# A matmul with leaky ReLU: a plain first unit, one ordered ring of rounding loads, stores on ScalarE, and two regions that take turns

## The chip, the cores and the metric

The kernel runs on one core of one Trainium2 chip; the other cores are idle. The metric is device time in microseconds (us), as the median of repeated runs.

## The reference

```python
def reference(a, b, alpha):          # a, b: 4096 x 4096 fp32, alpha 0.01
    x = np.matmul(a, b)
    return np.where(x > 0, x, alpha * x)
```

## The kernel before

The output is cut into regions of 512 x 1024 elements, 32 in all. A region fills the kernel's eight accumulator banks (4 row blocks `mt` by 2 column halves `nt`) and takes four units of 1024 along k, each of 8 slices `c`: 64 matmuls of 128x128 by 128x512 per unit and region, 8192 in all. Two regions in a row (`h` = 0, 1) share the same B. The kernel transposes A and rounds both inputs to bf16.

A came by GpSimd, whose transfers round on the way, and was transposed by VectorE. B came as fp32 over Sync's queue and was rounded by ScalarE (first region) or VectorE. Stores were issued by GpSimd too:

```python
    def load_a(mb, h, sub, mp):
        ...                                   # (cut) 256 rows of A, one unit
        for q in range(4):
            src = a[row:row + 2 * P, k0 + q * w:k0 + (q + 1) * w]
            nc.gpsimd.dma_start(a16[32 * q:32 * q + 32], src.rearrange("(g i) w -> i g w", i=32))
        ...
        nc.vector.transpose(dst..., a16...)   # (cut)

    def load_b(pi, n, sub, c, scalar=False):
        ...
        nc.sync.dma_start(b32, src[:, c, :])
        if scalar:
            nc.scalar.copy(bt[pi, u][:, c0 + c, :], b32)
        else:
            nc.vector.tensor_copy(bt[pi, u][:, c0 + c, :], b32)
    ...
    # end of a row block in the first two regions
                nc.gpsimd.dma_start(place(0, h, pairs[0], mt), o)
```

`TURNS = [[0, 1, 2, 3, 4]]` meant that the first region ran through all of k before the second began.

## Time and profile before

| | before |
|---|---|
| time, median of 3 runs | 1828.29 us (1827.49 to 1829.02) |
| span of the profiled run | 1825.7 us |

The prediction below reads the profile: only the first 140 us have room.

### The profile page before, as it was taken

The page shows a single profiled execution, that of the slowest core. Times are in us where ns is not written, and L with a number is a line of the kernel's source. Part 1 is how long each engine was busy: PE and PEld are TensorE (multiplying, and loading weights), DVE is VectorE, ACT ScalarE, POOL GpSimd, SP SyncE. Part 2 cuts the span into 40 slices and gives each one's busy share as a digit, 9 for nine tenths or more (in the row PEclk, how much of TensorE's full clock was granted, in tenths as well). Part 3 has the DMA queues.
Part 4 walks back from the last instruction along what each step waited for, and adds up shares of the span by engine and source line. Part 5 has one row for each costly group of instructions (what it writes and reads, how often), then busy time and mean ns, then how long its engine had stood idle before and what let it go on. Part 6 is the DMA issues. An engine that isn't in the chain of part 4 may idle for free.

```text
span 1825.7 us, 18868 instructions
## 1 busy us (share of the span) xinstructions
PE 1776.4 (97%) x8041; PEld 804.5 (44%) x8204; DVE 475.6 (26%) x465; ACT 174.3 (10%) x290; POOL 253.6 (14%) x448
## 2 busy tenths in 40 slices
PE   5789999999999999999999999999999999999999
PEld 2334444444444444444444444444444444444444
DVE  1454231214442213022452312201255130311000
ACT  5200000000000000000000000000000000000001
POOL 3150000033310000003520000001242000000000
PEclk7899999999999999999999999999999999999999
DMA  9799773465585629155856835617387581644111
GB/s 325 181 162 352 270 272 143 181 141 101 100 235 210 230 105 338 65 196 81 131 100 230 289 126 198 263 64 226 62 111 198 203 337 46 244 171 160 70 46 47
DMA packets 166037, 320.04 MB, mean 175 GB/s; under 512 B 46657, under 2 KB 95809, under 8 KB 165953
## 3 DMA queue, kind: packets, MB, share of 16 engines
q1 hardware_dynamic: 61056, 220.23, 33.0%
q0 software_dynamic: 104896, 98.59, 24.7%
q8 instruction: 64, 1.05, 0.2%
q14 instruction: 21, 0.16, 0.0%
HBM read 285.21 MB, written 67.11 MB: 193 GB/s over the span
## 4 chain that ended last, share of the span: by engine, by line
PE 93%; DMA 4%; issue 2%; POOL 1%; DVE 0%; ACT 0%; POOLq 0%; DVEq 0%
PE ps L101 93%; DMA a<-in_a_dram 4%; POOL a L81 0%; POOL out_dram L233 0%; DVE at L83 0%; ACT o L288 0%; DVEq L83 0%; POOLq L81 0%; POOLq L233 0%; POOLq L310 0%
## 5 line engine op out<-in xcount | busy, mean ns | idle before, releaser
L101 PE MATMUL ps<-bt,at 128*128 128x512 bf16 x8029 | 1772.1, 381 | 43.4 <-DVE at L83 34.7
L101 PEld LDWEIGHTS <-at 128*128 128x128 bf16 x8192 | 803.0, 98 | 1012.5 <-DVE at L83 40.2
L98 DVE CAST bt<-b 128x1024 bf16<-128x1024 f32 x384 | 256.6, 691 | 851.9 <-PE ps L101 553.0
L83 DVE STREAM_TRANSPOSE at<-a 128x2048 bf16<-128x2048 bf16 (+1 forms) x80 | 219.4, 2779 | 365.1 <-DMA a<-in_a_dram 241.9
L288 ACT ACTIVATE o<-ps 128x512 f32<-128x512 f32 x240 | 130.7, 595 | 1524.1 <-PE ps L101 1408.2
L292 POOL DMA_DIRECT2D out_dram<-o x116 | 64.5, 556 | 1364.8 <-ACT o L288 1355.8
L81 POOL DMA_DIRECT2D a<-in_a_dram x320 | 183.4, 587 | 83.4 <-DMA a<-in_a_dram 50.5
L96 ACT CAST bt<-b 128x1024 bf16<-128x1024 f32 x32 | 33.4, 1045 | 26.1 <-DMA b<-in_b_dram 26.1
L232 ACT ACTIVATE o<-ps 128x512 f32<-128x512 f32 x16 | 8.7, 594 | 97.4 <-PE ps L101 87.9
L233 POOL DMA_DIRECT2D out_dram<-o x8 | 5.5, 687 | 66.5 <-ACT o L232 66.5
L126 PE MATMUL ps<-w 128*128 128x512 bf16 x12 | 4.3, 532 | 2.3 <-ACT w L123 2.3
L126 PEld LDWEIGHTS <-w 128*128 128x128 bf16 x12 | 1.5, 131 | 4.6 <-ACT w L123 2.3
L123 ACT ACT_TABLE_LOAD x1 | 1.3, 1283 | 0.7 <-PEq L310 0.7
L122 DVE MEMSET w<- 128x256 uint32 x1 | 0.3, 272 | 0.9 <-PEq L310 0.9
L123 ACT ACTIVATE w<-w 128x8 bf16<-128x8 bf16 x1 | 0.2, 208 | 0.0
L310 POOL MEMSET const-float32-0.0<- 128x1 f32 x1 | 0.1, 98 | 0.2 <-issue 0.2
L310 POOL MEMSET const-bfloat16-1.0<- 128x1 bf16 x1 | 0.1, 101 | 0.0
L310 POOL MEMSET const-float32-1.0<- 128x1 f32 x1 | 0.1, 98 | 0.0
L310 POOL MEMSET const-uint8-127<- 128x1 uint8 x1 | 0.1, 98 | 0.0
## 6 DMA issues: line engine op xcount, KB each, us to landing
b<-in_b_dram SPq DMA_DIRECT2D x416, 512.0 KB, 5.4
out_dram<-o POOLq DMA_DIRECT2D x124, 512.0 KB, 2.9
a<-in_a_dram POOLq DMA_DIRECT2D x192, 128.0 KB, 5.1
a<-in_a_dram POOLq DMA_DIRECT2D x128, 64.0 KB, 3.3
out_dram<-o SPq DMA_DIRECT2D x8, 256.0 KB, 2.0
```

What stands on the lines that cost most here:

```text
L81: nc.gpsimd.dma_start(a16[32 * q:32 * q + 32], src.rearrange("(g i) w -> i g w", i=32))
L83: nc.vector.transpose(dst.rearrange("p c (g i) -> p g c i", g=8), a16.rearrange("p g (j c) -> p g c j", c=kc))
L96: nc.scalar.copy(bt[pi, u][:, c0 + c, :], b32)
L98: nc.vector.tensor_copy(bt[pi, u][:, c0 + c, :], b32)
L101: nc.tensor.matmul(ps, at[mb, h, u][:, c, mt * P:(mt + 1) * P], bt[pi, u][:, c, nt * NT:(nt + 1) * NT], start=first, stop=last,)
L123: nc.scalar.activation(w[:, :8], w[:, :8], LRELU, alpha=alpha)
L126: nc.tensor.matmul(wp, w[:, :P], w, start=True, stop=True)
L232: nc.scalar.activation(o[:, nt * NT:(nt + 1) * NT], done, LRELU, alpha=alpha)
L233: nc.gpsimd.dma_start(place(0, h, pairs[0], mt), o)
L288: nc.scalar.activation(o[:, cols], banks[mt, nt], LRELU, alpha=alpha)
L292: nc.gpsimd.dma_start(to, o)
L310: nc = _bacc.Bacc("TRN2", target_bir_lowering=False, num_devices=1)
```

## The change

Its intent: A and B share one queue, that of GpSimd, called the ring here, in the order in which they are needed; "plain" is a load that doesn't round; the first unit comes plain over Sync at once, its A turned by TensorE; the first two regions take turns over k, so that the same bytes feed twice the matmuls; stores leave GpSimd.

```diff
-TURNS = [[0, 1, 2, 3, 4]]
+TURNS = [[0], [1], [2, 3]]
...
     def load_b(...):
-        nc.sync.dma_start(b32, src[:, c, :])
-        ... ScalarE or VectorE rounds b32 into bt
+        nc.gpsimd.dma_start(new_b(pi, u)[:, c, :], b_rows(n, u, c))
...
+    order = [("a", 0), ("b", 0), ("a", 1), ("b", 1), ("b", 2), ("a", 2), ...]   # first unit, on nc.sync
+    def take(what, i):
+        if what == "b":
+            nc.scalar.copy(b0[:, i, :], b_in[i // 4][:, i % 4, :])
+            return
+        nc.vector.tensor_copy(a_rounded[:, i, :], a_in[:, i, :])
+        for c in range(KC):
+            nc.tensor.transpose(turned[i, c // 4][:, c % 4, :], cols[:, c, :], ident)
+        nc.scalar.copy(a0[:, :4, i * P:(i + 1) * P], turned[i, 0])
+        nc.vector.tensor_copy(a0[:, 4:, i * P:(i + 1) * P], turned[i, 1])
...
+        if (what, i) == ("b", 3):
+            nc.gpsimd.tensor_copy(x[:, :1], b0[:, 2, :1])      # GpSimd's loads start after this
...
+            if last:
+                todo = [(quarter, c) for c in range(KC)]
+            else:
+                todo = [(mt, c) for c in (2 * quarter, 2 * quarter + 1) for mt in range(MT)]
...
-                nc.gpsimd.dma_start(place(0, h, pairs[0], mt), o)
+            nc.scalar.dma_start(place(0, h, pairs[0], mt), o)
...
-                        nc.gpsimd.dma_start(to, o)
+                        nc.scalar.dma_start(to, o)
```

At the end of a turn the partial sums go to SBUF (`spill`), in the first turn as copies by ScalarE (`nt` = 0) and VectorE (`nt` = 1), later as VectorE adds. The first two regions become eight steps of 64 matmuls each. Left out of the cut above: the number of buffers changes (5 for 4 of A's loads, 5 for 6 of B's units), A's first pieces are larger, and the warm-up has 8 matmuls for 12.

More of the change, by code (lines that the diff above doesn't have):

```diff
@@ L6 @@
 from concourse._compat import with_exitstack
+from concourse.masks import make_identity
 P = 128
@@ L45 @@
     alpha = float(alpha)
-    KU = K // (KC * P)
+    KW = KC * P
+    KU = K // KW
     RM = MT * P
     RN = NP * NT
+    QW = KW // 4
     HALVES = 2
@@ L52 @@
     NB = N // RN
-    subs = [(0, 0, 4, 0), (0, 4, 4, 512)] + [(u, 0, 8, 1024 * u) for u in range(1, KU)]
-    subs_of = {u: [s for s in subs if s[0] == u] for u in range(KU)}
+    assert TURNS[0] == [0] and sorted(sum(TURNS, [])) == list(range(KU))
+    small_pool = ctx.enter_context(tc.tile_pool(name="small", bufs=1))
     at_pool = ctx.enter_context(tc.tile_pool(name="at", bufs=HALVES * KU))
-    bt_pool = ctx.enter_context(tc.tile_pool(name="bt", bufs=KU + 2))
-    a16_pool = ctx.enter_context(tc.tile_pool(name="a16", bufs=4))
@@ L61 @@
-    b32_pool = ctx.enter_context(tc.tile_pool(name="b32", bufs=4))
+    bt_pool = ctx.enter_context(tc.tile_pool(name="bt", bufs=KU + 1))
+    part_pool = ctx.enter_context(tc.tile_pool(name="part", bufs=2))
+    a16_pool = ctx.enter_context(tc.tile_pool(name="a16", bufs=5))
     o_pool = ctx.enter_context(tc.tile_pool(name="oo", bufs=2))
-    warm_pool = ctx.enter_context(tc.tile_pool(name="warm", bufs=1))
     psum_pool = ctx.enter_context(tc.tile_pool(name="psum", bufs=8, space=bass.MemoryType.PSUM))
+    ident = small_pool.tile([P, P], BF16, name="ident")
@@ L66, with new_a @@
+    make_identity(nc, ident)
     ctx.enter_context(tc.manual_schedule())
+    w = small_pool.tile([P, NT], BF16, name="w")
+    nc.vector.memset(w, 0.0)
+    x = small_pool.tile([P, 8], FP32, name="x")
+    nc.vector.memset(x, 0.0)
+    nc.scalar.activation(x, x, LRELU, alpha=alpha)
+    wp = psum_pool.tile([P, NT], FP32, name="ps")
+    for _ in range(8):
+        nc.tensor.matmul(wp, w[:, :P], w, start=True, stop=True)
     at = {}
     bt = {}
-    def load_a(mb, h, sub, mp):
-        u, c0, kc, k0 = sub
+    def new_a(mb, h, u):
@@ L74, in load_a @@
         if (mb, h, u) not in at:
             at[mb, h, u] = at_pool.tile([P, KC, RM], BF16, name="at")
-        row = (mb * HALVES + h) * RM + 2 * mp * P
-        w = 32 * kc
-        a16 = a16_pool.tile([P, 8, w], BF16, name="a16")
-        for q in range(4):
-            src = a[row:row + 2 * P, k0 + q * w:k0 + (q + 1) * w]
-            nc.gpsimd.dma_start(a16[32 * q:32 * q + 32], src.rearrange("(g i) w -> i g w", i=32))
-        dst = at[mb, h, u][:, c0:c0 + kc, 2 * mp * P:2 * (mp + 1) * P]
@@ L83, in load_a, with new_b @@
-        nc.vector.transpose(
-            dst.rearrange("p c (g i) -> p g c i", g=8), a16.rearrange("p g (j c) -> p g c j", c=kc)
-        )
-    def load_b(pi, n, sub, c, scalar=False):
-        u, c0, kc, k0 = sub
+        return at[mb, h, u]
+    def new_b(pi, u):
         if (pi, u) not in bt:
             bt[pi, u] = bt_pool.tile([P, KC, RN], BF16, name="bt")
-        b32 = b32_pool.tile([P, RN], FP32, name="b32")
-        src = b[k0:k0 + kc * P, n * RN:(n + 1) * RN].rearrange("(p c) n -> p c n", c=kc)
-        nc.sync.dma_start(b32, src[:, c, :])
-        if scalar:
-            nc.scalar.copy(bt[pi, u][:, c0 + c, :], b32)
-        else:
-            nc.vector.tensor_copy(bt[pi, u][:, c0 + c, :], b32)
+        return bt[pi, u]
@@ new lines, in load_a @@
+    def load_a(mb, h, u, mp):
+        dst = new_a(mb, h, u)[:, :, 2 * mp * P:2 * (mp + 1) * P]
+        row = (mb * HALVES + h) * RM + 2 * mp * P
+        a16 = a16_pool.tile([P, 8, QW], BF16, name="a16")
+        for q in range(4):
+            src = a[row:row + 2 * P, u * KW + q * QW:u * KW + (q + 1) * QW]
+            nc.gpsimd.dma_start(a16[32 * q:32 * q + 32], src.rearrange("(g i) w -> i g w", i=32))
+        nc.vector.transpose(
+            dst.rearrange("p c (g i) -> p g c i", g=8), a16.rearrange("p g (j c) -> p g c j", c=KC)
+        )
@@ L100, in mm, with b_rows, load_b @@
+    def b_rows(n, u, c):
+        src = b[u * KW:(u + 1) * KW, n * RN:(n + 1) * RN]
+        return src.rearrange("(p c) n -> p c n", c=KC)[:, c, :]
+    def load_b(pi, n, u, c):
+        nc.gpsimd.dma_start(new_b(pi, u)[:, c, :], b_rows(n, u, c))
     def mm(ps, mb, h, pi, u, mt, nt, c, first, last):
@@ L118, in place @@
         return out[row:row + P, n * RN:(n + 1) * RN]
-    w = warm_pool.tile([P, NT], BF16, name="w")
-    nc.vector.memset(w, 0.0)
-    nc.scalar.activation(w[:, :8], w[:, :8], LRELU, alpha=alpha)
-    wp = psum_pool.tile([P, NT], FP32, name="ps")
-    for _ in range(12):
-        nc.tensor.matmul(wp, w[:, :P], w, start=True, stop=True)
     regions = []
@@ L142 @@
         for u in range(KU):
-            pieces = [
-                lambda pi=pi, sub=sub, c=c: load_b(pi, pairs[pi], sub, c)
-                for sub in subs_of[u]
-                for c in range(sub[2])
-            ]
             lead = 2 if pi == 1 else KU
-            loads.setdefault(first * KU + u - lead, []).extend(pieces)
+            loads.setdefault(first * KU + u - lead, []).extend(
+                lambda pi=pi, u=u, c=c: load_b(pi, pairs[pi], u, c) for c in range(KC)
+            )
     for mb in range(1, MB):
@@ L153 @@
             for u in range(KU):
-                pieces = [
-                    lambda mb=mb, h=h, sub=sub, mp=mp: load_a(mb, h, sub, mp)
-                    for sub in subs_of[u]
-                    for mp in range(MT // 2)
-                ]
-                loads.setdefault(first * KU + h * KU + u - 2 * KU + 1, []).extend(pieces)
-    def issue(slot, part):
-        pieces = loads.get(slot, [])
-        for piece in pieces[len(pieces) * part // 4:len(pieces) * (part + 1) // 4]:
+                loads.setdefault(first * KU + h * KU + u - 2 * KU + 1, []).extend(
+                    lambda mb=mb, h=h, u=u, mp=mp: load_a(mb, h, u, mp) for mp in range(MT // 2)
+                )
@@ L165, in issue, with quarter_of, step_loads @@
+    def quarter_of(pieces, quarter):
+        for piece in pieces[len(pieces) * quarter // 4:len(pieces) * (quarter + 1) // 4]:
             piece()
     steps = [
-        (t, h, sub, i == len(turn) - 1)
+        (t, h, u, i == 0, i == len(turn) - 1)
         for t, turn in enumerate(TURNS)
         for h in range(HALVES)
-        for i, sub in enumerate(turn)
+        for i, u in enumerate(turn)
     ]
-    def step_loads(t, h, si):
-        sub = subs[si]
+    def step_loads(h, u):
         if h:
-            return [lambda mp=mp: load_a(0, 1, sub, mp) for mp in range(MT // 2)]
-        order = "abbabb" if sub[2] == 4 else "abbbabbbbb"
-        made, na, nb = [], 0, 0
-        for what in order:
-            if what == "a":
-                made.append(lambda mp=na: load_a(0, 0, sub, mp))
-                na += 1
-            else:
-                made.append(lambda c=nb: load_b(0, pairs[0], sub, c, True))
-                nb += 1
-        return made
@@ L190 @@
-    queue = [step_loads(t, h, si) for t, h, si, _ in steps]
-    part = {}
-    if len(TURNS) > 1:
-        for piece in queue[0]:
-            piece()
-        queue[0] = []
-    banks = None
-    for i, (t, h, si, last) in enumerate(steps):
-        u, c0, kc, _ = subs[si]
-        for piece in queue[i]:
-            piece()
-        following = queue[i + 1] if i + 1 < len(steps) else []
-        queue[i] = []
-        if si == TURNS[t][0]:
-            banks = new_banks()
-        def go(mt, c):
-            for nt in range(NP):
-                mm(banks[mt, nt], 0, h, 0, u, mt, nt, c0 + c, si == TURNS[t][0] and c == 0,
-                   last and c == kc - 1)
-        def spill(mt):
-            if not last:
-                return
-            for nt in range(NP):
-                ps = banks[mt, nt]
-                if len(TURNS) == 1:
-                    continue
-                if h not in part:
-                    part[h] = bt_pool.tile([P, MT, NP, NT], FP32, name="part", tag="bt")
-                kept = part[h][:, mt, nt, :]
-                if t == 0:
-                    if h == 0 and nt:
-                        nc.vector.tensor_copy(kept, ps)
-                    else:
-                        nc.scalar.copy(kept, ps)
-                else:
-                    nc.vector.tensor_add(kept, ps, kept)
-            if t == len(TURNS) - 1:
-                o = o_pool.tile([P, RN], FP32, name="o")
-                for nt in range(NP):
-                    done = banks[mt, nt] if len(TURNS) == 1 else part[h][:, mt, nt, :]
-                    nc.scalar.activation(o[:, nt * NT:(nt + 1) * NT], done, LRELU, alpha=alpha)
-                nc.gpsimd.dma_start(place(0, h, pairs[0], mt), o)
-        def ahead(quarter):
-            for piece in following[len(following) * quarter // 4:len(following) * (quarter + 1) // 4]:
-                piece()
-        extra = len(steps) - 2
-        if i == 0:
-            for mts, cs in (((0, 1), (0, 1)), ((2, 3), (0, 1)), ((0, 1, 2, 3), (2, 3))):
-                for c in cs:
-                    for mt in mts:
-                        go(mt, c)
-            for quarter in range(4):
-                ahead(quarter)
-                spill(quarter)
-        elif last:
-            for mt in range(MT):
-                for c in range(kc):
-                    go(mt, c)
-                spill(mt)
-                ahead(mt)
-                if i >= extra:
-                    issue(2 * KU - 2 + i - extra, mt)
-        else:
-            for quarter in range(4):
-                for c in range(kc * quarter // 4, kc * (quarter + 1) // 4):
-                    for mt in range(MT):
-                        go(mt, c)
-                ahead(quarter)
-                if i >= extra:
-                    issue(2 * KU - 2 + i - extra, quarter)
-        if i + 1 < len(steps):
-            queue[i + 1] = []
@@ new lines, in step_loads, with spill @@
+            return [lambda mp=mp: load_a(0, 1, u, mp) for mp in range(MT // 2)]
+        made = [lambda c=c: load_b(0, pairs[0], u, c) for c in range(KC)]
+        made.insert(4, lambda: load_a(0, 0, u, 1))
+        made.insert(0, lambda: load_a(0, 0, u, 0))
+        return made
+    queue = [step_loads(h, u) for _, h, u, _, _ in steps]
+    part = {}
+    def spill(t, h, mt, banks):
+        for nt in range(NP):
+            kept = part[h][:, mt, nt * NT:(nt + 1) * NT]
+            if t == 0:
+                if nt:
+                    nc.vector.tensor_copy(kept, banks[mt, nt])
+                else:
+                    nc.scalar.copy(kept, banks[mt, nt])
+            else:
+                nc.vector.tensor_add(kept, banks[mt, nt], kept)
+        if t == len(TURNS) - 1:
+            o = o_pool.tile([P, RN], FP32, name="o")
+            nc.scalar.activation(o, part[h][:, mt, :], LRELU, alpha=alpha)
+            nc.scalar.dma_start(place(0, h, pairs[0], mt), o)
@@ new lines @@
+    a_in = bt_pool.tile([P, MT, KW], FP32, name="a_in", tag="bt")
+    b_in = [part_pool.tile([P, KC // 2, RN], FP32, name="b_in", tag="part") for _ in range(2)]
+    a_rounded = at_pool.tile([P, MT, KW], BF16, name="a_rounded", tag="at")
+    order = [("a", 0), ("b", 0), ("a", 1), ("b", 1), ("b", 2), ("a", 2), ("b", 3), ("a", 3),
+             ("b", 4), ("b", 5), ("b", 6), ("b", 7)]
+    for what, i in order:
+        if what == "a":
+            nc.sync.dma_start(a_in[:, i, :], a[i * P:(i + 1) * P, :KW])
+        else:
+            nc.sync.dma_start(b_in[i // 4][:, i % 4, :], b_rows(pairs[0], 0, i))
@@ new lines @@
+    a0 = new_a(0, 0, 0)
+    b0 = new_b(0, 0)
+    turned = {
+        (mt, i): psum_pool.tile([P, KC // 2, P], BF16, name="turned", tag="ps")
+        for mt in range(MT)
+        for i in range(2)
+    }
+    banks = new_banks()
+    def take(what, i):
[3 more added lines that the diff above has]
+        nc.vector.tensor_copy(a_rounded[:, i, :], a_in[:, i, :])
+        cols = a_rounded[:, i, :].rearrange("m (p c) -> m c p", c=KC)
+        for c in range(KC):
+            nc.tensor.transpose(turned[i, c // 4][:, c % 4, :], cols[:, c, :], ident)
+        nc.scalar.copy(a0[:, :4, i * P:(i + 1) * P], turned[i, 0])
+        nc.vector.tensor_copy(a0[:, 4:, i * P:(i + 1) * P], turned[i, 1])
@@ new lines @@
+    there = {"a": [], "b": []}
+    ready = []
+    begun = set()
+    for n, (what, i) in enumerate(order):
+        take(what, i)
+        if (what, i) == ("b", 3):
+            nc.gpsimd.tensor_copy(x[:, :1], b0[:, 2, :1])
+        there[what].append(i)
+        now = [(i, c) for c in there["b"]] if what == "a" else [(mt, i) for mt in there["a"]]
+        ready.append(now)
+        for mt, c in ready[n - 1] if n else []:
+            for nt in range(NP):
+                mm(banks[mt, nt], 0, 0, 0, 0, mt, nt, c, (mt, nt) not in begun, False)
+                begun.add((mt, nt))
@@ new lines @@
+    for piece in queue[1]:
+        piece()
+    part[0] = part_pool.tile([P, MT, RN], FP32, name="part", tag="part")
+    for mt, c in ready[-1]:
+        for nt in range(NP):
+            mm(banks[mt, nt], 0, 0, 0, 0, mt, nt, c, False, True)
+        spill(0, 0, mt, banks)
+    for piece in queue[2]:
+        piece()
+    for i in range(1, len(steps)):
+        t, h, u, first, last = steps[i]
+        following = queue[i + 1] if 2 <= i and i + 1 < len(steps) else []
+        own = 2 * KU - 2 + i - (len(steps) - 2)
+        if first:
+            banks = new_banks()
+            if h not in part:
+                part[h] = part_pool.tile([P, MT, RN], FP32, name="part", tag="part")
+        for quarter in range(4):
+            if last:
+                todo = [(quarter, c) for c in range(KC)]
+            else:
+                todo = [(mt, c) for c in (2 * quarter, 2 * quarter + 1) for mt in range(MT)]
+            for mt, c in todo:
+                for nt in range(NP):
+                    mm(banks[mt, nt], 0, h, 0, u, mt, nt, c, first and c == 0,
+                       last and c == KC - 1)
+            if last:
+                spill(t, h, quarter, banks)
+            quarter_of(following, quarter)
+            if own >= 2 * KU - 2:
+                quarter_of(loads.get(own, []), quarter)
@@ L276 @@
                 if final and last:
-                    order = [(c, nt) for nt in range(NP) for c in range(KC)]
+                    todo = [(c, nt) for nt in range(NP) for c in range(KC)]
                 else:
-                    order = [(c, nt) for c in range(KC) for nt in range(NP)]
-                for c, nt in order:
+                    todo = [(c, nt) for c in range(KC) for nt in range(NP)]
+                for c, nt in todo:
                     mm(banks[mt, nt], mb, h, pi, u, mt, nt, c, u == 0 and c == 0,
@@ L291 @@
                     if not final:
-                        nc.gpsimd.dma_start(to, o)
-                issue(r * KU + u, mt)
+                        nc.scalar.dma_start(to, o)
+                quarter_of(loads.get(r * KU + u, []), mt)
 _INS = ['a', 'b', 'alpha']
```

## The prediction

The sum came to 25 us lost: 16.2 ahead of the second step, and three terms, estimates of 3.0 us ahead of the fifth step, 4.3 ahead of the seventh and 1.5 for the half clock after it. In the 30.3 us for the second step, 0.3 and 0.7 are estimates as well; the kernel before has 0.69 us for a cast on VectorE.

> **What bounds the kernel now.** I read the page's totals and slices first, then the table of windows, the timeline of TensorE and the list of waits over the first 140 us.
>
> ```profile
> span 1825.7 us, 18868 instructions
> ...
> PE   5789999999999999999999999999999999999999
> PEld 2334444444444444444444444444444444444444
> ...
> PEclk7899999999999999999999999999999999999999
> ```
>
> Each digit is the busy share of 1/40 of the span (45.6 us). Only the first three slices are not full: nothing can be won in the other 37. The table of windows (columns: PE busy and count, PEld busy and count, DVE, ACT, POOL, granted clock, DMA share, GB/s) puts a number on it:
>
> ```profile
> 0.00:140.00 140.00, 102.44 (x404) 42.55 (x413) 56.89 (x27) 39.26 (x42) 48.33 (x88) 0.85 0.94 223
> 140.00:1826.00 1686.00, 1673.93 (x7639) 761.94 (x7791) 418.72 (x439) 135.02 (x248) 205.24 (x360) 1.00 0.55 171
> ...
> 400.00:600.00 200.00, 199.06 (x910) 90.60 (x927) 79.11 (x58) 14.67 (x28) 43.83 (x77) 1.00 0.65 162
> ```
>
> I count weight loads, because some matmul records are missing: 927 in 200 us is 0.2157 us per matmul. The 8192 matmuls need 8192 x 0.2157 = 1767 us. The first 140 us hold 413 loads less 12 of the warm-up = 401, worth 86.5 us, so **53.5 us are lost there**. After 140 us 7791 loads are worth 1680.5 of 1685.7 us: 5.2 us, nearly all of it the tail after the last matmul. 1767 + 53.5 + 5.2 = 1825.7, the span. The change can win back at most the 53.5 us, and in practice not the wait for the first data.
>
> What TensorE waits for there, from its timeline (start, duration, then in brackets the idle time before and its releaser):
>
> ```profile
> 12.20 3.58 PE L101 MATMUL ps<-bt,at 128*128 128x512 bf16 x8 [5.63 <-DVE at L83]
> 18.34 7.90 PE L101 MATMUL ps<-bt,at 128*128 128x512 bf16 x28 [2.56 <-DVE at L83]
> ...
> 43.42 1.89 PE L101 MATMUL ps<-bt,at 128*128 128x512 bf16 x4 [3.90 <-DVE at L83]
> 54.50 16.70 PE L101 MATMUL ps<-bt,at 128*128 128x512 bf16 x63 [9.20 <-DVE at L83]
> ...
> 108.22 32.06 PE L101 MATMUL ps<-bt,at 128*128 128x512 bf16 x137 [6.13 <-DVE at L83]
> ```
>
> VectorE is only the messenger. It transposes A and itself waits for A's transfers, as the waits of that window say:
>
> ```profile
> DVE at L83 <- DMA a<-in_a_dram: 82.2, 13, 19.4
> POOL a L81 <- DMA a<-in_a_dram: 46.2, 25, 2.9
> ```
>
> So A is starved while B flows on the other queue. In the timeline the ScalarE casts of B between 20 and 60 us follow each other every 1.65 us (512 KB, 318 GB/s), while the transposes of A start at 39.55, 50.63, 62.45 us: 1 MB of fp32 per 11.5 us, about 90 to 105 GB/s. B takes three to four times A's share, and A is needed first. Also, one region needs 24 MB for 55 us of matmuls, while two regions need 32 MB for 110 us: with one region at a time the DMA is the limit, with two it is not.
>
> [...] B's packets are 4 KB and A's 1 KB of source, and the bytes divide about 3 or 4 to 1. One ring removes this. [...] after the 9.20 us of idle the matmuls at 54.50 us come 0.43 us apart until 60.0 us; after a 1.7 us gap at 72.91 us they stay at 0.216. [...]
>
> **The change, part by part.**
>
> *Casts of B.* 384 on VectorE (256.6 us) and 32 on ScalarE (33.4 us) go. From 140 us on TensorE waits for neither: worth nothing in the steady part. Matmuls and their order there stay as they were: 1767 us.
>
> *B by GpSimd's ring.* Can the ring carry it? A's rounding loads alone moved 192 GB/s written between 120 and 125 us, 384 GB/s read, and the plain B loads 359 GB/s between 140 and 200 us. I take 360 GB/s read for both: a B row is 4 KB in and 2 KB out, no smaller than A's pieces, so I see no reason for less. Issue costs 0.57 us of GpSimd each, 512 KB per 1.46 us at that rate: hidden.
>
> *First unit plain, on Sync.* 6 MB in 12 transfers of 512 KB at 1.4 us each, first landing about 4.2 us (the first cast of the old kernel starts at 4.55). VectorE rounds A (0.69 us), TensorE does 32 transposes. Matmuls follow arrivals, cold at first. The order of instructions on GpSimd shows that the ring starts only after ScalarE has copied the third B slice: landing 9.8 us plus 1.05 us and a queue behind A's copies, about 12 us. From then it shares with the last four or five plain loads, at 1.65 us each: the plain unit is in at 20.6 us. TensorE has 64 x 0.216 = 13.8 us of matmuls[...] from 7.8 us on, some cold: I put its end at 27 us.
>
> *Second step (other half of A, same B).* The ring's first 1 MB gets about 105 GB/s until 20.6 us and is in at 21.7. The instruction order on VectorE puts both transposes of 3.82 us (row 128x2048) ahead of its copies of the first partial sums, and TensorE needs the first such copy for a free bank: 21.7 + 0.3 + 7.6 + 0.7 = 30.3, so **step 2 begins at about 30 us** where ideally it is 13.8: 16.2 us lost.
>
> *Further steps.* 64 matmuls are 13.8 us each, eight steps in all. Step 3 starts at 44: its 6 MB stand behind the second 2 MB (in at 24.5), so in at 24.5 + 17.5 = 42: just in time. After that the ring needs 8 MB / 0.36 = 23.3 us per unit against 27.6 us of matmuls and runs ahead. What is left is VectorE, which works in program order. In step 4 (counting from one) it has eight adds[...] and three transposes: one left over from step 3, two for step 5. [...] At the end of step 6 the last add[...] is followed by a transpose that step 7 needs for its fifth matmul[...]. Steps 2 to 4 otherwise find their data.
>
> *Stores* move from GpSimd (0.556 us each) to ScalarE, 0.60 us x 2 of work per 3.45 us: off the path.
>
> [...] Span 1767 + 25 + 5.2 = 1797.2; the old kernel's time exceeds its span by 2.6 us, so about **1800 us**; I choose 1799. The gain is 29 us of the 53.5, 1.6%.
>
> **Rivals.** *(a) VectorE does not hold TensorE up:* if the copies and adds end early enough, or the ring gets more than a quarter beside Sync so that step 2 begins at 27, only 13 to 15 us are lost: 1767 + 14 + 5.2 + 2.6 = 1789. For: VectorE is busy only 26% now. Against: the instruction order. *(b) The rounding B loads are slow,* say 250 GB/s read. Then the 21 MB of steps 3 to 8 that follow 24.5 us, with A at 360, take about 76 us instead of 58, and the last B unit lands near 105 us rather than 85, when step 6 wants it at 89: 15 us more, 1815. For: the trace of before holds no such transfer. Against: A's smaller pieces run at 384. *(c) The ring in order becomes a bound later,* a store or A load blocking B: B then is asked for four units (55 us) ahead and takes 16 MB / 0.36 = 46 us, and the A loads of the next rows fall in regions that load no B. I expect nothing, at worst a few us.
>
> **Range and chances.** 2% faster begins at 1828.3 / 1.02 = 1792.4; it needs the losses to be 18 us or less, that is rival (a). My central value is 7 us above; I give it 0.25. Slower needs over 90 us of loss: 0.02. Range 1788 to 1809: (a) whole on one side, half of (b) on the other.
>
> **What would show it.** Right: weight loads 0.216 us apart from 140 us on; no releaser "DMA b" on TensorE after the first unit; TensorE idle ahead of steps 2, 5 and 7 with VectorE as releaser[...]; first 64 matmuls done at 25 to 29 us; DMA share high until about 100 us. Wrong: TensorE waiting for B's transfers in steps 3 to 6 (the ring's rate), or gaps after 140 us (the ring's order), or no gaps ahead of steps 5 and 7 (my reading of VectorE's list).

## More of the kernel before

One more view of the kernel before matters for what follows, and the prediction did not use it: the timeline of GpSimd around the end of the first region. The columns are start, duration, engine, line, operation and tiles, count, and in brackets the idle time before and what ended it; L233 is the output store, L81 the loads of A.

```profile
90.69 0.57 POOL L233 DMA_DIRECT2D out_dram<-o  x1 [20.90 <-ACT o L232]
94.14 0.55 POOL L233 DMA_DIRECT2D out_dram<-o  x1 [2.88 <-ACT o L232]
94.69 2.32 POOL L81 DMA_DIRECT2D a<-in_a_dram  x4
...
101.10 0.55 POOL L233 DMA_DIRECT2D out_dram<-o  x1 [2.88 <-ACT o L232]
101.99 7.99 POOL L81 DMA_DIRECT2D a<-in_a_dram  x14 [0.35 <-issue]
```

GpSimd sat 20.9 us in front of a store whose result was not there yet, and the loads of A for the second region stood behind it.

## The result

The changed kernel took **1795.59 us** (1793.4 to 1796.25, 4 runs) against 1827.89 (1826.87 to 1829.02, 4 runs): ratio 0.9821, 95% interval 0.9804 to 0.9838. Ratios are from runs of the same rounds, and are not quite the ratio of the medians quoted. The saving is 32.3 us, 1.8%: clear of the noise, but short of the 2% from which the record calls a kernel faster.

The page of the changed kernel, totals and slices:

```profile
span 1794.5 us, 17965 instructions
...
PE   8999999999999999999999999999999999999999
PEld 4434444444444444444444444444444444444444
...
PEclk9999999999999999999999999999999999999999
```

The first slice is now nearly full and the next two are full to the eye. The table of windows, as before (PE busy and count, PEld busy and count, DVE, ACT, POOL, granted clock, DMA share, GB/s):

```profile
0.00:140.00 140.00, 128.64 (x573) 58.04 (x585) 82.05 (x64) 24.44 (x30) 67.79 (x126) 0.98 1.16 231
140.00:1795.00 1655.00, 1642.83 (x7496) 748.24 (x7647) 182.22 (x48) 130.68 (x240) 292.94 (x538) 1.00 0.54 110
400.00:600.00 200.00, 199.00 (x910) 90.64 (x927) 41.41 (x11) 16.39 (x31) 37.13 (x68) 1.00 0.56 113
```

The pace is the same, 927 loads in 200 us. In the first 140 us there are 585 loads less 8 of the warm-up and 32 of the transposes, 545, worth 117.6 us: **22.4 us lost instead of 53.5**. After that 7647 are worth 1649.5 of 1654.5 us: 5.0 us, as before. So the whole gain is in the first two regions. Where the 22.4 us are, TensorE's timeline says:

```profile
10.00 3.62 PE L116 MATMUL ps<-bt,at 128*128 128x512 bf16 x8
...
16.70 10.09 PE L116 MATMUL ps<-bt,at 128*128 128x512 bf16 x45
27.39 42.48 PE L116 MATMUL ps<-bt,at 128*128 128x512 bf16 x193 [0.60 <-ACT part L193]
71.40 0.73 PE L116 MATMUL ps<-bt,at 128*128 128x512 bf16 x2 [1.54 <-DVE at L103]
72.35 27.14 PE L116 MATMUL ps<-bt,at 128*128 128x512 bf16 x123 [0.22 <-DVE part L195]
103.50 56.78 PE L116 MATMUL ps<-bt,at 128*128 128x512 bf16 x244 [4.00 <-DVE at L103]
```

The second step begins at 27.39 us, 13.6 us later than if matmuls had begun at zero. Steps 2 to 4 run without a gap. Ahead of the fifth step the stretch from 69.87 to 72.35 us holds two matmuls, so about 2.0 us are lost; in the seventh 4.00 us. After that gap the weight loads come 0.43 us apart from 103.5 to 109.4 us, 14 of them, so the half clock costs 14 x 0.21 = 2.9 us (granted clock 0.51 in that stretch). 13.6 + 2.0 + 4.0 + 2.9 = 22.5. The recorded clock does not show every slow stretch: it is 1.00 from 10.0 to 13.4 us, where the eight matmuls from 10.00 us take 3.62 us, 0.43 us apart. VectorE (DVE) is the releaser at both gaps, and its timeline shows why; L103 is the transpose of A, L195 the adds:

```profile
60.04 1.24 DVE L195 TENSOR_TENSOR part<-ps,part 128x512 f32<-128x512 f32 x2
61.20 3.83 DVE L103 STREAM_TRANSPOSE at<-a 128x2048 bf16<-128x2048 bf16 x1
64.96 2.44 DVE L195 TENSOR_TENSOR part<-ps,part 128x512 f32<-128x512 f32 x4
67.31 3.80 DVE L103 STREAM_TRANSPOSE at<-a 128x2048 bf16<-128x2048 bf16 x1
71.04 1.26 DVE L195 TENSOR_TENSOR part<-ps,part 128x512 f32<-128x512 f32 x2
...
98.45 1.29 DVE L195 TENSOR_TENSOR part<-ps,part 128x512 f32<-128x512 f32 x2 [0.65 <-PE ps L116]
99.66 11.19 DVE L103 STREAM_TRANSPOSE at<-a 128x2048 bf16<-128x2048 bf16 x3
```

There is no idle time in it from 60 to 72 us. The last transpose for the fifth step starts at 67.31 and ends at 71.1 us, where TensorE's wait ends; the last one for the seventh is the first of the three from 99.66 us, and ends at about 103.4.

The list of waits in the first 140 us has for A:

```profile
POOL bt L113 <- DMA bt<-in_b_dram: 34.7, 39, 2.3
...
DVE at L103 <- DMA a<-in_a_dram: 6.0, 1, 6.0
```

VectorE waited once for a transfer of A from the ring, 6.0 us, and 6.5 us in three for the plain ones of the first unit, against 82.2 us in 13 times before. What counts is TensorE: its waits for transposed A fell from 34.7 to 5.5 us. GpSimd waits for its own transfers: its timeline while it loads B alone shows an issue about each 1.25 us, each after a slice of 512 KB has landed.

```profile
112.01 0.54 POOL L113 DMA_DIRECT2D bt<-in_b_dram  x1 [0.70 <-DMA bt<-in_b_dram]
113.24 0.54 POOL L113 DMA_DIRECT2D bt<-in_b_dram  x1 [0.69 <-DMA bt<-in_b_dram]
114.49 0.54 POOL L113 DMA_DIRECT2D bt<-in_b_dram  x1 [0.72 <-DMA bt<-in_b_dram]
115.79 0.54 POOL L113 DMA_DIRECT2D bt<-in_b_dram  x1 [0.76 <-DMA bt<-in_b_dram]
```

512 KB (524,288 bytes) of fp32 in 1.25 us is 419 GB/s read.

### The profile page after: what moved, and what is told of

It reads as the page before. It is cut to its first block, busy times and chain, and to the rows that moved or that the text cites. A ratio compares the mean times of both kernels' runs of the same rounds, so it can differ in the third digit from the quotient of the medians.

```text
span 1794.5 us, 17965 instructions
## 1 busy us (share of the span) xinstructions
PE 1771.5 (99%) x8068; PEld 806.3 (45%) x8232; DVE 264.3 (15%) x112; ACT 155.1 (9%) x270; POOL 360.7 (20%) x663
## 4 chain that ended last, share of the span: by engine, by line
PE 97%; DMA 2%; issue 1%; DVE 0%; ACT 0%; POOL 0%; SPq 0%; DVEq 0%; POOLq 0%
PE ps L116 97%; DMA a<-in_a_dram 1%; DMA a_in<-in_a_dram 0%; DVE at L103 0%; DVE part L195 0%; PE turned L228 0%; ACT part L193 0%; POOL a L102 0%; DVE a_rounded L225 0%; ACT o L300 0%; SPq L211 0%; SPq L209 0%; DVEq L195 0%; POOLq L102 0%
## 5 line engine op out<-in xcount | busy, mean ns | idle before, releaser
L113 POOL DMA_DIRECT2D bt<-in_b_dram x408 | 217.3, 539 | 1097.4 <-PE ps L116 908.0
L103 DVE STREAM_TRANSPOSE at<-a 128x2048 bf16<-128x2048 bf16 x62 | 235.6, 3842 | 1046.0 <-PE ps L116 1033.7
L300 ACT ACTIVATE o<-ps 128x512 f32<-128x512 f32 x240 | 130.7, 595 | 1524.6 <-PE ps L116 1462.5
L102 POOL DMA_DIRECT2D a<-in_a_dram x248 | 142.3, 579 | 201.3 <-DVE at L103 142.8
L195 DVE TENSOR_TENSOR part<-ps,part 128x512 f32<-128x512 f32 x32 | 20.3, 680 | 33.7 <-PE ps L116 31.6
L198 ACT ACTIVATE o<-part 128x1024 f32<-128x1024 f32 x8 | 8.5, 1057 | 86.0 <-DVE part L195 79.2
L223 ACT CAST bt<-b_in 128x1024 bf16<-128x1024 f32 x8 | 8.1, 1045 | 2.2 <-DMA b_in<-in_b_dram 2.0
L193 ACT COPY part<-ps 128x512 f32<-128x512 f32 x8 | 4.4, 594 | 14.2 <-PE ps L116 14.2
L191 DVE COPY part<-ps 128x512 f32<-128x512 f32 x8 | 5.2, 838 | 0.0
```

Of the source, the lines that this page charges most:

```text
L103: nc.vector.transpose(dst.rearrange("p c (g i) -> p g c i", g=8), a16.rearrange("p g (j c) -> p g c j", c=KC))
L113: nc.gpsimd.dma_start(new_b(pi, u)[:, c, :], b_rows(n, u, c))
L191: nc.vector.tensor_copy(kept, banks[mt, nt])
L193: nc.scalar.copy(kept, banks[mt, nt])
L195: nc.vector.tensor_add(kept, banks[mt, nt], kept)
L198: nc.scalar.activation(o, part[h][:, mt, :], LRELU, alpha=alpha)
```

## The experiments

The theory after the result: the gain comes from A no longer starving beside B, that is from the one ring; the rest that is lost is VectorE's order of work. The rivals: the turns carry the gain; the plain first unit does; the stores do. Four kernels, called the ladder below, build the change up from the kernel before, one takes the turns after the first unit out of the changed kernel and one puts the stores back, and the others test the gaps and the start. All ratios, also those of kernels edited from the changed one, are against the kernel before in their own rounds. Differences in us between kernels are of medians; where the rounds differ they hold to about 1 us, as the kernel before itself came out at 1827.89 to 1828.76 us.

### Stores on ScalarE, nothing else

```diff
-                nc.gpsimd.dma_start(place(0, h, pairs[0], mt), o)
+                nc.scalar.dma_start(place(0, h, pairs[0], mt), o)
-                        nc.gpsimd.dma_start(to, o)
+                        nc.scalar.dma_start(to, o)
```

> The kernel before with one part of the change: output stores issued by ScalarE instead of GpSimd. Theory (stores are off the path): 1828 us, within 1 us of before, and the 53.5 us lost in the first 140 us unchanged. Rival (stores standing in A's ring delay A in the second region, where TensorE waits 6.13 us at 108 us): 3 to 6 us less.

Measured: 1819.72 us against 1828.22, ratio 0.9955 (0.994 to 0.997): **8.5 us less**, so the theory fell and the rival was right, and by more than it said. TensorE's timeline at the end of the first region:

```profile
72.85 28.23 PE L101 MATMUL ps<-bt,at 128*128 128x512 bf16 x127 [0.90 <-DVE at L83]
101.50 58.71 PE L101 MATMUL ps<-bt,at 128*128 128x512 bf16 x265 [0.41 <-ACT o L232]
```

The 6.13 us of idle ahead of 108.22 us in the kernel before, and the half clock after it (weight loads 0.43 us apart until 111.2 us, granted clock 0.50), are gone. The loads of A for the second region now start at about 70 us instead of 94.69.

### B in the ring as well, still one region at a time

```diff
-        nc.sync.dma_start(b32, src[:, c, :])
-        ... rounding by ScalarE or VectorE
+        nc.gpsimd.dma_start(bt[pi, u][:, c0 + c, :], src[:, c, :])
```
(with the stores on ScalarE)

> The kernel before with stores on ScalarE and B loaded by rounding GpSimd transfers in program order with A's; still one region at a time. Theory A (the gain of the change is the one ring, because A is no longer starved, and in the changed kernel's trace the ring moves a 512 KB slice of B each 1.25 us, 419 GB/s read): 24 MB are in about 63 to 68 us after the start, the first region ends by about 72, so 17 to 20 us lost in all and 1793 to 1800 us. Rival B (the turns are what matters, since one region alone asks for more bytes than it has matmuls to cover): 1810 to 1820 us.

Measured: 1799.14 us, ratio 0.9842 (0.9827 to 0.9856), 20.6 us less than with the stores alone. Theory A's time holds, rival B falls; the 17 to 20 us lost that went with it were too few, 25.3 us are lost in the first 140. The end of TensorE's waits in this kernel:

```profile
36.23 31.61 PE L95 MATMUL ps<-bt,at 128*128 128x512 bf16 x133 [5.01 <-DVE at L82]
68.45 0.59 PE L95 MATMUL ps<-bt,at 128*128 128x512 bf16 x2 [0.60 <-DMA bt<-in_b_dram]
70.02 90.16 PE L95 MATMUL ps<-bt,at 128*128 128x512 bf16 x409 [0.98 <-DMA bt<-in_b_dram]
```

From 70.02 us on there is no gap. One region at a time does wait for B, but the waits are about 1 us long, 3.8 us in four.

The edit also ends the casts and changes the rate, which are rivals of the order. The trace speaks against both. With the stores alone TensorE waited for no cast in the first 140 us. And between 20 and 60 us that kernel read 302 GB/s over Sync and 90 over GpSimd (12.07 MB and twice 1.79 MB, as a rounding load writes half of what it reads), some 391 in all; the ring read 402. The bytes come hardly faster, but in the order of need: the first three transposes of 256 rows by 1024 of A start at 25.91, 32.41 and 42.11 us, where they started at 40.12, 51.68 and 63.29, and TensorE's waits for them fall from 27.1 to 9.4 us.

### Turns, with B still on Sync

```diff
-TURNS = [[0, 1, 2, 3, 4]]
+TURNS = [[0, 1], [2], [3, 4]]
```
(with the stores on ScalarE)

> The kernel before with stores on ScalarE and the two first regions taking turns, B still plain on Sync with casts on ScalarE. Theory A (starvation of A beside Sync stays): A still gets about 105 GB/s while B flows, 1808 to 1825 us. Rival B (turns suffice, since they halve what is needed per us): 1795 to 1802 us.

Measured: 1813.01 us, ratio 0.9915 (0.99 to 0.993), 6.7 us less than with the stores alone, inside theory A's range. Its trace doesn't show theory A alone, though. ScalarE casts no B from 17.5 to 43.7 us, because the next casts stand in its program order behind the copies of the second region's partial sums; Sync moves nothing between 26 and 46 us; and from 49 to 58 us TensorE waits for the casts, 5.3 us in five. So the 6.7 us are what these turns gave with B held up by another engine's order. What turns would give beside a starved A without that was not tried.

### Ring and turns

Both edits and the stores, with one more buffer for the partial sums.

> Both together: one ring and turns, without the plain first unit and without TensorE transposes. Theory A: about as the changed kernel, 1790 to 1800 us, as the plain first unit saves only the first few us (its first matmul came at 10 us against 12.2 before) and the turns add VectorE adds. Rival C (the plain first unit is worth much, as GpSimd's issue of 64 KB pieces at 0.57 us each holds up the ring): 1800 to 1808 us.

Measured: 1801.77 us, ratio 0.9857 (0.984 to 0.9873), 1.8 us above theory A's range and inside rival C's, though rival C's reason, the issue of small pieces, was not tested. It is 2.6 us slower than the ring without turns: the turns bring the spills, and TensorE waits 4.2 us for VectorE ahead of 109.7 us, as the changed kernel does. The changed kernel is 6.2 us faster than this one. This step holds the plain first unit, but also larger pieces of A and another order of spills, so the 6.2 us belong to these together.

### The changed kernel with no turns after the first unit

```diff
-TURNS = [[0], [1], [2, 3]]
+TURNS = [[0], [1, 2, 3]]
```

> The changed kernel with the turns after the first unit taken out: the first region does units 1, 2 and 3, then the second region does. Theory (with the ring at 419 GB/s read, turns are hardly needed): the first region waits some 2 us for B of the last unit, the second begins with the same VectorE wait of 4 us and 3 us of half clock: 1793 to 1799 us. Rival (turns carry a large part of the gain): over 1802 us.

Measured: 1794.87 us, ratio 0.9814 (0.9799 to 0.9828), against 0.9821 for the changed kernel: the same within the intervals. Theory holds, for the turns after the first unit; the first unit still takes its turn here. TensorE waited for B 0.2 us in the first 140 us, once, where I had said 2 us, and 4.06 us for VectorE ahead of 89.24 us.

### The changed kernel with the stores back on GpSimd

> The changed kernel with its output stores put back on GpSimd. Theory (a store that waits for its result holds up, on the same in-order engine, the A loads written after it): the seventh step's last A load is issued only after the fourth store of the sixth step, near 101 us, so its transpose ends at about 109 instead of 103.5 us: 5 to 8 us more, 1800 to 1804 us. Rival (the ring is far enough ahead for stores to cost nothing there): 1795 to 1797 us.

Measured: 1813.66 us, ratio 0.9916 (0.99 to 0.9933), **18 us more** than the changed kernel; the direction of the theory was right and its size was less than half. TensorE's timeline:

```profile
104.62 1.89 PE L116 MATMUL ps<-bt,at 128*128 128x512 bf16 x4 [6.68 <-DVE at L103]
120.59 39.69 PE L116 MATMUL ps<-bt,at 128*128 128x512 bf16 x170 [14.08 <-DVE at L103]
```

and GpSimd's, L199 being the stores and L102 A's loads:

```profile
93.53 0.54 POOL L199 DMA_DIRECT2D out_dram<-o  x1 [2.92 <-ACT o L198]
94.10 2.32 POOL L102 DMA_DIRECT2D a<-in_a_dram  x4
107.16 0.56 POOL L199 DMA_DIRECT2D out_dram<-o  x1 [10.74 <-ACT o L198]
108.36 0.55 POOL L199 DMA_DIRECT2D out_dram<-o  x1 [0.63 <-ACT o L198]
108.91 0.60 POOL L102 DMA_DIRECT2D a<-in_a_dram  x1
```

It is a circle. The third store waits for the adds of the third row block; these stand on VectorE behind the transpose of an A load, and that load was itself issued only after the second store. The last A load then waits for the third and the fourth store. I had counted only the last link of it. The 20.8 us of idle in the seventh step are 16.8 us more than the 4.00 in the changed kernel, and the clock drops as it does there (0.50 from 104 to 121 us here, 0.51 from 103.5 to 109.4 there). So the ring in order pays in full only if nothing stands in it that waits for a result: in this run GpSimd, which issues, sat out the wait, 10.74 us in front of one store, and the loads written after it waited too.

### Row order in the fifth and seventh step

```diff
-            if last:
-                todo = [(quarter, c) for c in range(KC)]
-            else:
-                todo = [(mt, c) for c in (2 * quarter, 2 * quarter + 1) for mt in range(MT)]
+            todo = [(quarter, c) for c in range(KC)]
```

> The changed kernel with one edit: the two steps that are not last in their turn (fifth and seventh) also go row block by row block, so that they need the last transposes and the last freed banks 7 to 10 us later. Theory (VectorE's list in program order is what holds TensorE at 71 and 103 us, and the half clock after the second gap costs 3 us more): 1.8 + 4.0 + 3.0 = 8.8 us less, about 1787 us, and the clock whole in 100 to 110 us. Rival (the gaps are the DMA's in disguise: B or A come late): the wait moves to DMA and the time stays within 2 us of the changed kernel.

Measured: **1786.2 us**, ratio 0.977 (0.9755 to 0.9784), 9.4 us less than the changed kernel. TensorE's timeline to 160 us ends in one stretch:

```profile
27.80 132.48 PE L116 MATMUL ps<-bt,at 128*128 128x512 bf16 x601 [0.49 <-DVE at L103]
```

Both gaps and the half clock are gone (601 matmul records in 132.48 us, 0.22 us each), and no wait for a transfer came in their place: the theory holds and the rival falls. VectorE does the same work in the same order; TensorE merely asks for the last row block later.

### Each accumulator its own bank

```diff
-            (mt, nt): psum_pool.tile([P, NT], FP32, name="ps")
+            (mt, nt): psum_pool.tile([P, NT], FP32, name="ps", tag=f"ps{mt}{nt}")
```
(the same tags for the warm-up tile and the transposes' tiles, and one buffer for each tag)

> The changed kernel with one edit: each of the eight accumulators has its own bank for good, where the shared pool hands out the banks that ScalarE frees first. My prediction took banks to be fixed like this. Theory (that assumption is the whole of my error on the second step): the second step does one or two matmuls at 27.4 us, then waits for VectorE's copy at about 31.5 us, 4 us idle and up to 3 us of half clock: 1799 to 1803 us. Rival (the order of banks does not matter): 1795 to 1796 us.

Measured: 1800.24 us, ratio 0.9844 (0.9827 to 0.986). TensorE's timeline:

```profile
28.18 0.39 PE L116 MATMUL ps<-bt,at 128*128 128x512 bf16 x1 [1.92 <-DVE at L103]
32.41 44.29 PE L116 MATMUL ps<-bt,at 128*128 128x512 bf16 x192 [3.84 <-DVE part L191]
```

One matmul, then 3.84 us until VectorE's copy of the first partial sum, as the theory said. With the shared pool the changed kernel has no such wait. Its instruction order says why, by my reading: the first four accumulators of the second step wait for ScalarE alone, as the pool had given them the four banks that ScalarE's copies free, and those copies do not stand behind VectorE's transposes. The releaser at 27.39 us, ScalarE's copy L193, fits that.

### An earlier ring, alone and with row order

```diff
-        if (what, i) == ("b", 3):
-            nc.gpsimd.tensor_copy(x[:, :1], b0[:, 2, :1])
+        if (what, i) == ("b", 1):
+            nc.gpsimd.tensor_copy(x[:, :1], b0[:, 0, :1])
```

> The changed kernel with the ring released by the copy of the first B slice (about 7.5 us) instead of the third (12.4 us). Theory (the second step is held by the landing of its first 1 MB of A, but the first step ends only 0.6 us before): A comes 4 to 5 us sooner, the plain loads end about 1 us later, so the second step begins at 27 to 28.5 us and the time is 1795 to 1797 us. Rival (A alone holds the start): 2 to 4 us less.

Measured: 1795.38 us, ratio 0.9817 (0.9802 to 0.9832), as the theory said: no difference from the changed kernel.

> Row order and early ring together. Theory (with the gaps gone, the start of the second step sets the end, and the early ring moved that from 27.4 to 26.4 us): 1785 to 1786 us, 0 to 1.5 us less than row order alone. Rival (the early ring only delays the plain loads): 1786 to 1788 us.

Measured: 1787.42 us, ratio 0.9772 (0.9758 to 0.9787), the rival's range; nothing over row order alone (0.977). The second step began at 27.59 us.

### And a longer warm-up

```diff
-    for _ in range(8):
+    for _ in range(16):
```

> The same with 16 instead of 8 warm-up matmuls, to about 6 to 7 us, so that [...]the first eight real matmuls, which take 3.6 us at half clock, run at full clock. Theory (TensorE is busy without a gap from 14 us to the end of the first step, so the 1.7 us come off the end): 1783.5 to 1785 us. Rival (the transposes of the other half of A, ending at about 26 us, hold the second step): no gain, 1785 to 1786 us; or the warm-up delays the first transposes and it is 1 us worse.

Measured: 1786.74 us, ratio 0.9769 (0.9754 to 0.9783): no gain that the intervals show. The first eight matmuls did run at full clock but for a wait of 0.34 us between them, and the first step's last stretch of matmuls ended at 25.7 us in the trace, against 27.0 with 8, but TensorE then waited 0.98 us for the transposed A at 26.66 us. Of the three versions at 1786 to 1787 us, row order alone is the one to keep, being one line.

## Why the prediction was right, and where it was not

The time was right: 1799 said, 1795.6 measured, inside the range, with 22.4 us lost against 25 said. The 2% that it gave a chance of 0.25 was not reached. By its own steps:

**The sum of matmuls** (1767 us) and the tail (5.2 us, measured 5.0) held, and nothing was gained or lost after 140 us.

**The starvation of A** held, and the ladder shows it: with the stores already moved, one ring alone took 20.6 us. The shares were read a little off: 23 casts of B in 40 us are 1.74 us apart, not 1.65, and by the bytes of 20 to 60 us B had 298 GB/s and A 92, three to one. The ring's rate was mis-sized, 419 GB/s read for 360, on the safe side.

**"Stores … off the path" was wrong.** This is the step that failed. I looked at what a store costs to issue, 0.556 us, and not at what stands behind it while it waits. Moving them is worth 8.5 us in the kernel before, and putting them back costs 18 us in the changed one. The total came out right all the same, for this part by luck: I gave all 53.5 us to A's starvation, the change happened to take the stores out of the ring, and I predicted what would remain rather than what each part takes away.

**"With one region at a time the DMA is the limit, with two it is not"** was right in its bytes and wrong in what it is worth. At 419 GB/s the 24 MB of one region need 60 us for 55 us of matmuls, so little is left to wait for. The ring without turns gave 1799.14 us, with turns 1801.77; the changed kernel without those after the first unit 1794.87, with them 1795.59. Only with B still on Sync did they take something off, 6.7 us. Whether they are worth something once row order has closed VectorE's gaps was not tried.

**The second step** was to start at 30.3 us and started at 27.39, so 13.6 us were lost where the sum has 16.2 (from a rounded 30; by 30.3 it is 16.5). VectorE's list was read nearly right here too: its first copy of a partial sum starts at 30.88 us, behind both transposes. The term that failed is the first free bank: I took it that each accumulator comes back to its own bank, so that TensorE would wait some 3 us for that copy. It waited 0.60 us, and for ScalarE. Where the own bank is forced, the step starts in earnest at 32.41 us.

**VectorE's list** was right in both places. Ahead of the fifth step I said 3.0 us and it was about 2.0. The 3.0 was an estimate with a time for the adds that no trace had shown. In the changed kernel a pair of adds takes 1.16 to 1.20 us of the list and a transpose 3.73 to 3.76. One add lasts 0.680 us on average; but they overlap a little, and four in a row took 2.44 us, 0.61 each.

In the seventh step I said 4.3 us, an estimate of the same kind, and it was 4.00. The half clock after it cost 2.9 us where I said about 1.5, which no trace had shown either. The trace before spoke against it: the matmuls at 54.50 us, which the prediction quotes, took 5.5 us to get the clock back (granted clock 0.50), though those at 108.22 us took 3.0. After the 4.00 us gap it was 5.9.

Half of rival (a) came true at once, as the second step began near 27 us; row order did the rest, 9.4 us: the rival names 1789 us, and the kernel with row order takes 1786.2. Rival (b) fell with the ring's rate (its sum was too dark as well: the 21 MB are those of steps 3 to 6, 12.6 of B and 8.4 of A, about 74 us at its rates, so some 9 us late and not 15), and rival (c) too, as no gap came after 140 us.

Built up in the order of the ladder, by the medians, the gain of some 32 us is: stores 8.5, ring 20.6, turns 2.6 lost, and 6.2 for the plain first unit with what came along with it. In another order the shares differ, as the 18 us of the stores show. What of the 6.2 us is the plain transfer alone stays open. So does the rest of the start, some 13 to 14 us in the changed kernel and in the versions with row order.

## What to carry to other kernels

Before calling a transfer off the path, look at what its issuing engine does next: here a store that waited for its result, for 20.9 us in the kernel before and 10.74 with the stores put back, held up the loads written after it on the same engine, and one ordered ring of loads is only as good as the waits that are kept out of it. When a bottleneck engine works through a fixed list, ask not only how long the list is but which consumer needs its last entry first; letting TensorE ask for it later was one line and gave 9.4 us more. And check in which order a shared pool gives buffers out before counting a wait for one.
